# An encoder layer on one core: where a Strassen unit is split, when column sums are taken, which engine empties PSUM

## The chip, the cores and the metric

The kernel runs on one core of one Trainium2 chip. The metric is the time of one execution on the device in microseconds (us). The chip's engines work side by side, each through its own queue in order: TensorE (PE: matmuls; PEld: its weight loads), VectorE (DVE), ScalarE (ACT), GpSimd (POOL) and SyncE (SP, which issues most DMAs). They wait for each other by semaphores.

## The reference

One encoder layer over 512 tokens of width 1024, in float32. `ffn1` and `ffn2` have an inner width of 2816, 22 tiles of 128.

```python
h = h + 0.5 * swiglu(rms_norm(h, g_ffn1), w_ffn1_gate, w_ffn1_up, w_ffn1_down)
u = rms_norm(h, g_mix) @ w_in
h = h + concat([mla(u), diff_attention(u)]) @ w_out      # 8 + 4 heads
h = h + 0.5 * swiglu(rms_norm(h, g_ffn2), w_ffn2_gate, w_ffn2_up, w_ffn2_down)
gate = sigmoid(rms_norm(h, g_ple_in) @ w_ple_gate + b_ple_gate)
h = h + gate * rms_norm(p @ w_ple_proj, g_ple_out)       # p: 512 x 256, the "embedding"
```

## The kernel before

Activations lie transposed: 8 tiles `h[m]` of 128 features x 512 tokens. A float32 product is made of three matmuls (`mm3`, L407): each operand is split into a high part, a cast on ScalarE (`cast`), and a low part, the rest, a subtraction on VectorE (`low`, recorded at L97; where the helper `split` makes both, L93 and L94). High x high, high x low and low x high are summed in PSUM; these are the matmul lines L408, L409 and L410.

**The feed-forward block** (`ffn`, L590) goes through its 22 inner tiles in four groups (`FGROUPS`). Group 0 has four plain tiles: for each a gate and an up projection of 24 matmuls each, then `evac` (L598: scaling, Silu, product, and the split into `ht`), then the down projection (`ps_d`) for the 8 output tiles m; of the first three (`heads`, L668) all but the last tile's share is done ahead. Groups 1 to 3 have six tiles each, worked in pairs by `seven` (L550): one level of Strassen's scheme, seven products `r` of 256 columns in place of eight. Its weight side, a `Unit` (L135), needs sums of weight blocks: loads `ra`, `rb`, `rc`; two accumulating DMAs on POOL's queue (`sums`); then eleven steps in all of casts and lows to `xa`, `xb`, `xc`, `xs`, with two additions on POOL (L174, L175). Its activation side, `Forms` (L491), is made in group 0 by `build`, a generator that is advanced a few steps at a time beside the projections: per half, four products `y`, two POOL subtractions (`n1`, `n3`, L523 and L524), the splits `sa` of the four `y`, and the splits `fm` of four forms N1, T2, N3, N4, with `t2_` (L529) and `n4` (L532) made on VectorE.

**The order of the work.** In these blocks the program order on PE, DVE, ACT and POOL is kept as it is written (`manual_schedule`); in the attention only PE's is, and the scheduler places the rest. All weights of the kernel stand in one list, `items`: a `Chunk` (one tile: cast, low) or a `Unit`. `nxt` hands out the next finished one and frees the one used before. `slot(us)` spends a budget of VectorE time on the next steps of the list (`advance`, which stops when three tiles of a pool are held: `held`), and it stands at given places between the matmuls, ahead of the evacuation of the product just made; `load_ahead` issues loads while fewer than three raw tiles are in flight. The first unit of the next group is cut in two `Part`s of one and four steps (`cut`, L220), put among the down chunks, so that its sums start early. In group 0 both parts stand between the second and the third of four down chunks, and the four steps (`cast_a`, `low_a`, `cast_b`, `low_b`) come up in the slot behind the up projection of the last plain tile (L653), ahead of its `evac`.

**The column sums of the embedding.** `embed` (L964) makes p @ w_ple_proj in the attention, eight tiles of 6 matmuls; each leaves PSUM by a vector copy into a t2 tile (L981) and goes to DRAM by a POOL DMA (L982). A table, `FILL_STEPS`, says after which attention step a tile is made: 6, 8, ... 20 in this kernel. The tiles `pT` (the split p) stay in four t2 tiles of 16 until the last. In FFN2, `pe_norm` (L473) loads the eight tiles back (`pel`), squares them on ScalarE, adds the squares on POOL (`pe_acc`, L354), and at its last step takes the column sums by eight small matmuls (`ps_ss`, L364). It is advanced by two steps after each m of group 1's down projection (L701), so that its last step comes after m = 5.

**The end.** The gate is made in eight tiles; `evac_gate` (L1263) is three vector operations, a sigmoid and the store. The last tile is made in three pieces of 256, 128 and 128 columns (L1287).

Of the kernel before, what the change touches and what calls it, by code (L numbers as in the profile page):

```python
# [8 lines left out]
F32 = mybir.dt.float32  # L9
# [6 lines left out]
S = 512  # L16
DM = 1024
KT = DM // P
TT = S // P
# [16 lines left out]

FILL_PRE = "TTTTTTTTTTTTTKTKTKTTT"
FILL_MID = "TKK"
FILL_STEPS = ("T", "TTE", "TT", "TT", "T", "") + ("E", "") * 8
HEADS = "DDMDMDMMMMMM"  # L40

GC = {"ffn1": 0, "mix": 8, "ffn2": 16, "ple_in": 24, "ple_out": 32, "b_ple": 40,
# [7 lines left out]
def encoder_layer(ctx, tc, xT, pT, wst, gcols, rows, consts, out):  # L50
    nc = tc.nc
# [24 lines left out]
    def t2(name, dt=F32):  # L76
        return scope["t2p"].tile([P, S], dt, tag="t2", name=name)

    def page(name, shape=(P, 2, S), dt=F32R, pool=None):
        return (pool or pgp).tile(list(shape), dt, tag="pg", name=name)  # L80
# [8 lines left out]
    UP = (768, 768, BLK)  # L89
    st = {"off": P * sum(UP), "raws": 0, "time": 0.0}  # L90

    def split(dst_h, dst_l, src):
        nc.scalar.copy(dst_h, src)  # L93
        nc.vector.tensor_sub(dst_l, src, dst_h.bitcast(F32))  # L94

    def sub(dst_l, src, dst_h):
        nc.vector.tensor_sub(dst_l, src, dst_h.bitcast(F32))  # L97
# [114 lines left out]
    items = []  # L212

    def ffn_items():
        first_unit = None
        for gi, (f0, n, plain) in enumerate(FGROUPS):
            if plain:
                items.extend(Chunk(BLK) for _ in range(2 * n))
                down = [Chunk(2 * n * P) for m in range(0, KT, 2)]
                cut = 2, 2  # L220
            else:
                items.extend(first_unit if u == 0 else Unit(1 - u % 2) for u in range(n))
                down = [Chunk(n * P, 1 if m < KT // 2 else 0) for m in range(KT)]
                cut = 6, 7
            if gi < len(FGROUPS) - 1:
                first_unit = Unit(1)
                early_ = Part(first_unit, 1, 2), Part(first_unit, 4, 0)
                down.insert(cut[1], early_[1])
                down.insert(cut[0], early_[0])
            items.extend(down)  # L230
# [34 lines left out]
        load_ahead()  # L265
        return True

    def slot(us):

        st["time"] = us  # L270
        load_ahead()
        while st["time"] > 0 and (not any(isinstance(it, Unit) for it in ready)
                                  or isinstance(items[-1], Unit) and len(items[-1].steps) == 11) and advance():
            pass

    def steps(n):
# [214 lines left out]
    class Forms:  # L491
# [10 lines left out]
        def build(self, kp):  # L502
            def v(t):
                return t.rearrange("p (a b) -> p a b", b=HS)

            def put(i, src):
                pg_ = page(f"fm{i}")
                d = pg_.rearrange("p x (a b) -> p x a b", b=HS)
                split(d[:, 0], d[:, 1], src)
                self.pg[kp][i] = pg_  # L510

            held[1] += 1
            y = hl_tile(1, "y", F32)
            ks = (2 * kp, 2 * kp + 1, 2 * kp + 4, 2 * kp + 5)
            for i, k in enumerate(ks):
                nc.vector.scalar_tensor_tensor(out=y[:, i // 2, (i % 2) * S:(i % 2 + 1) * S], in0=h[k],
                                               scalar=g(self.name, k), in1=self.rbc, op0=ALU.mult, op1=ALU.mult)
                yield
            q = [y[:, i].rearrange("p (a b) -> p a b", b=S) for i in range(2)]
            b11, b12 = q[0][:, :, :HS], q[0][:, :, HS:]  # L520
            b21, b22 = q[1][:, :, :HS], q[1][:, :, HS:]
            n1, t2_, n3, n4 = [v(t2(f"f{i}")) for i in range(4)]
            nc.gpsimd.tensor_sub(n1, b11, b12)  # L523
            nc.gpsimd.tensor_sub(n3, b12, b22)  # L524
            for i, k in enumerate(ks):
                self.sa[k] = page(f"sa{k}")
                split(self.sa[k][:, 0, :], self.sa[k][:, 1, :], y[:, i // 2, (i % 2) * S:(i % 2 + 1) * S])
                yield
            nc.vector.tensor_add(t2_, b22, n1)  # L529
            put(self.N1, n1)  # L530
            yield
            nc.vector.tensor_sub(n4, b21, t2_)  # L532
            put(self.T2, t2_)
            yield
            put(self.N3, n3)
            yield
            put(self.N4, n4)
            held[1] -= 1
            yield
# [50 lines left out]
    def ffn(norm, after, side=None, early=None):  # L590
# [46 lines left out]
        for gi, (f0, n, plain) in enumerate(FGROUPS):  # L637
            hts = []
            if plain:
                late = []  # L640
                for f in range(n):
                    if f == 0 and early is not None:
                        psg, psu = early
                    else:
                        psg = psum("ps_g")
                        proj(psg, nxt(), norm.act)
                        slot(5.4)
                        if f == 1:
                            st_["r4"] = col_rsqrt(norm.acc, DM)
                        build(2)  # L650
                        psu = psum("ps_u")
                        proj(psu, nxt(), norm.act)
                        slot(3.5)  # L653
                    late.append((psg, psu, hts))
                    if f == 1:
                        st_["rbc"] = row_bcast(st_["r4"])
                        forms = Forms(norm.name, st_["rbc"])
                        builder = (x for kp in range(2) for x in forms.build(kp))
                    if f > 0:
                        for e in late:  # L660
                            evac(*e)
                        late = []
                        build(3 if f == 1 else 4)
            else:
                build(99)
                for f in range(0, n, 2):
                    pair(hts)
            heads = []  # L668
            if plain:

                w = nxt()
                for m in range(3):
                    if m == 2:
                        while not ready:
                            advance()
                        w = ready[0].out
                    heads.append(psum("ps_d"))
                    proj(heads[m], w, hts, m % 2 * n, range(n - 1))
                    slot(1.3)
                    build(1)  # L680
                w = used[0].out
            for m in range(KT):
                if not plain:
                    ps = psum("ps_d")
                    proj(ps, nxt(), hts)
                else:
                    if m % 2 == 0 and m > 0:
                        w = nxt()
                    if m < 3:
                        ps = heads[m]  # L690
                        proj(ps, w, hts, m % 2 * n, range(n - 1, n))
                    else:
                        ps = psum("ps_d")
                        proj(ps, w, hts, m % 2 * n)
                slot(0.0 if plain and m < 2 else 0.68 * n - (2.2 if gi == len(FGROUPS) - 1 else 0.75))
                nc.vector.scalar_tensor_tensor(out=h[m], in0=ps, scalar=0.5, in1=h[m],
                                               op0=ALU.mult, op1=ALU.add)
                last = gi == len(FGROUPS) - 1
                if last:
                    after(m)  # L700
                elif side is not None and gi == 1:  # L701
                    for _ in range(2):
                        next(side, None)
                build(1 if m < 2 else 2)
# [259 lines left out]
    def embed():  # L964
        pa = []
        for k in range(2):
            pt_ = t2("pT")
            nc.sync.dma_start(out=pt_, in_=pT[k])
            ah, al = t2("pTh", F32R), t2("pTl", F32R)
            split(ah, al, pt_)  # L970
            pa.append((ah, al))
        yield
        for m in range(KT):
            if m % 4 == 0:
                w = chunk()
            ps = psum("ps_pe")
            for k in range(2):
                c = slice(((m % 4) * 2 + k) * P, ((m % 4) * 2 + k + 1) * P)
                mm3(ps, w[:, 0, c], w[:, 1, c], pa[k][0], pa[k][1], k == 0, k == 1)
            pe = t2("pe")  # L980
            nc.vector.tensor_copy(out=pe, in_=ps)  # L981
            nc.gpsimd.dma_start(out=pe_dram[m], in_=pe)  # L982
            yield

    side = cols()
# [298 lines left out]
            evac_gate(*e)  # L1284
        pend = []
    w = nxt()
    for c in (slice(0, 256), slice(256, 384), slice(384, 512)):  # L1287
        ps = psum("ps_pg")
        for k in range(KT):
            b = slice(k * P, (k + 1) * P)  # L1290
            mm3(ps[:, c], w[:, 0, b], w[:, 1, b], n3.act[k][:, 0, c], n3.act[k][:, 1, c], k == 0, k == KT - 1)
        evac_gate(KT - 1, ps, c)
# [112 lines left out]
```

## Time and profile before

| | us |
|---|---|
| three runs: median (lowest to highest) | 1062.23 (1060.98 to 1063.0) |
| the profiled execution | 1061.28 |
| its span, first to last instruction | 1059.5 |
| PE busy in the span | 1026.2 |
| DVE busy | 762.8 |
| ACT busy | 524.3 |
| POOL busy | 325.1 |

A profile shows when each instruction of one execution began and how long it took. "Idle before" is the time for which its engine had nothing running ahead of it, and the releaser is the instruction that ended the wait. The granted clock is TensorE's: 1.00 is 2.4 GHz, 0.50 is 1.2 GHz. Matmuls overlap in their records (0.39 us for one of 512 columns), so a pitch is read from start to start. Where a row says x3, three instructions are merged and the duration is from the first start to the last end.

### The profile page before, as it was taken

What the parts mean: (1) busy time and instruction counts of PE and PEld (TensorE: products, weight loads), DVE (VectorE), ACT (ScalarE), POOL (GpSimd) and SP (SyncE); (2) the same over time, 40 slices, a digit from 0 to 9 for tenths busy, and PEclk for the clock granted to TensorE, in tenths of its full rate; (3) what the DMA queues carried; (4) which work ended last, traced back from release to release, by engine and by line L of the source; (5) the groups of instructions that cost most, each with busy time, mean ns of one, the idle gap of its engine ahead of it and who ended that gap; (6) DMA issues with size and microseconds to landing.
All of it is one profiled execution on the core that took longest, in us unless ns stands there. A gap on an engine that the chain in (4) does not pass through costs nothing.

```text
span 1059.5 us, 16005 instructions
## 1 busy us (share of the span) xinstructions
PE 1026.2 (97%) x6100; PEld 899.0 (85%) x6100; DVE 762.8 (72%) x1277; ACT 524.3 (49%) x891; POOL 325.1 (31%) x283
## 2 busy tenths in 40 slices
PE   9969999999999999999999999979997999999998
PEld 7859998998999898876667888769986998999877
DVE  7778855886586659778798763898854875587764
ACT  7435533543354457577687543445542562344441
POOL 1233412432341300036553221234415531352000
PEclk9989999999999999999899999989998999999999
DMA  6245654755563541321111123346574655565321
GB/s 242 99 121 163 158 164 110 181 149 167 132 160 118 170 163 60 96 79 51 60 49 62 41 81 98 95 114 160 142 218 119 154 143 180 140 160 180 120 100 50
DMA packets 50461, 133.76 MB, mean 126 GB/s; under 512 B 5872, under 2 KB 6896, under 8 KB 50384
## 3 DMA queue, kind: packets, MB, share of 16 engines
q1 hardware_dynamic: 37008, 106.88, 30.2%
q0 software_dynamic: 11792, 23.47, 12.7%
q10 hardware_dynamic: 1584, 2.39, 0.6%
q8 instruction: 48, 0.79, 0.3%
q14 instruction: 29, 0.24, 0.1%
HBM read 126.02 MB, written 6.29 MB: 125 GB/s over the span
## 4 chain that ended last, share of the span: by engine, by line
PE 81%; DVE 8%; ACT 4%; DMA 4%; issue 2%; POOL 1%; SPq 0%; ACTq 0%; DVEq 0%; POOLq 0%
PE r L410 11%; PE r L408 11%; PE r L409 11%; PE ps_d L408 7%; PE ps_d L409 6%; PE ps_d L410 6%; PE ps_in L408 2%; PE ps_in L410 2%; PE ps_in L409 2%; DVE hl L97 1%; PE ps_pt L1160 1%; PE ps_wo L408 1%; PE ps_wo L410 1%; PE ps_wo L409 1%; PE ps_pg L409 1%
## 5 line engine op out<-in xcount | busy, mean ns | idle before, releaser
L97 DVE TENSOR_TENSOR hl<-raw,hl 128x1024 fp32r<-128x1024 f32 (+4 forms) x110 | 121.4, 1116 | 69.2 <-ACT hl L124 66.9
L408 PE MATMUL ps_d<-ht,hl 128*128 128x512 f32 x352 | 140.3, 398 | 13.5 <-ACT ht L93 13.5
L124 ACT CAST hl<-raw 128x1024 fp32r<-128x1024 f32 (+2 forms) x104 | 96.4, 942 | 98.6 <-DMA raw<-in_wst_dram 28.8
L410 PE MATMUL ps_d<-ht,hl 128*128 128x512 f32 x352 | 139.1, 395 | 1.8 <-DVE hl L97 1.8
L409 PE MATMUL ps_d<-ht,hl 128*128 128x512 f32 x352 | 139.5, 396 | 0.0
L174 POOL TENSOR_TENSOR ra<-ra,rb 128x512 f32<-128x512 f32 x36 | 48.3, 1341 | 224.2 <-DVE xa L97 216.2
L408 PEld LDWEIGHTS ps_d<-ht,hl 128*128 128x128 f32 x352 | 67.6, 192 | 28.1 <-ACT ht L93 14.3
L410 PEld LDWEIGHTS ps_d<-ht,hl 128*128 128x128 f32 x352 | 67.4, 192 | 16.8 <-DVE hl L97 2.6
L408 PE MATMUL r<-sa,xa 128*128 128x256 f32 x288 | 81.5, 283 | 0.0
L409 PE MATMUL r<-sa,xa 128*128 128x256 f32 x288 | 81.5, 283 | 0.0
L410 PE MATMUL r<-sa,xa 128*128 128x256 f32 x288 | 81.5, 283 | 0.0
L408 PE MATMUL r<-fm,xb 128*128 128x256 f32 x288 | 81.5, 283 | 0.0
L409 PE MATMUL r<-fm,xb 128*128 128x256 f32 x288 | 81.5, 283 | 0.0
L410 PE MATMUL r<-fm,xb 128*128 128x256 f32 x288 | 81.5, 283 | 0.0
L409 PEld LDWEIGHTS ps_d<-ht,hl 128*128 128x128 f32 x352 | 67.6, 192 | 14.7 <-DVE ht L94 0.9
L175 POOL TENSOR_TENSOR ra<-ra 128x512 f32<-128x512 f32 x36 | 75.0, 2084 | 2.8
L97 DVE TENSOR_TENSOR xa<-ra,xa 128x1024 fp32r<-128x1024 f32 x36 | 44.3, 1231 | 38.7 <-ACT xa L162 38.7
L157 POOL DMA_DIRECT2D rb<-in_wst_dram x36 | 31.7, 882 | 110.7 <-DMA rb<-in_wst_dram 89.2
L97 DVE TENSOR_TENSOR xb<-rb,xb 128x1024 fp32r<-128x1024 f32 x36 | 63.1, 1753 | 0.0
L408 PEld LDWEIGHTS r<-sa,xa 128*128 128x128 f32 x288 | 55.3, 192 | 0.0
L409 PEld LDWEIGHTS r<-sa,xa 128*128 128x128 f32 x288 | 55.3, 192 | 0.0
L410 PEld LDWEIGHTS r<-sa,xa 128*128 128x128 f32 x288 | 55.3, 192 | 0.0
(335 smaller groups left out, 3047.3 us busy)
## 6 DMA issues: line engine op xcount, KB each, us to landing
raw<-in_wst_dram SPq DMA_DIRECT2D x52, 512.0 KB, 3.5
rb<-in_wst_dram SPq DMA_DIRECT2D x36, 512.0 KB, 3.8
ra<-in_wst_dram SPq DMA_DIRECT2D x36, 512.0 KB, 3.5
raw<-in_wst_dram SPq DMA_DIRECT2D x48, 384.0 KB, 3.1
rc<-in_wst_dram SPq DMA_DIRECT2D x36, 256.0 KB, 4.7
rb<-in_wst_dram POOLq DMA_DIRECT2D x36, 256.0 KB, 4.9
rc<-in_wst_dram POOLq DMA_DIRECT2D x36, 256.0 KB, 5.8
h<-in_xT_dram SPq DMA_DIRECT2D x8, 256.0 KB, 4.8
```

The costliest lines, as they stand in the source:

```text
L97: nc.vector.tensor_sub(dst_l, src, dst_h.bitcast(F32))
L124: nc.scalar.copy(self.hl[:, 0, :self.n], self.raw[:, :self.n])
L157: nc.gpsimd.dma_start(out=self.rb[:, self.LO], in_=self.s1[:, self.HI], accum_op=ALU.add)
L174: nc.gpsimd.tensor_add(ra[:, LO], ra[:, LO], self.rb[:, LO])
L175: nc.gpsimd.tensor_add(ra[:, HI], ra[:, HI], ra[:, LO])
L408: MM(ps, lhsT=wh, rhs=ah, start=start, stop=False, **kw)
L409: MM(ps, lhsT=wh, rhs=al, start=False, stop=False, **kw)
L410: MM(ps, lhsT=wl, rhs=ah, start=False, stop=stop, **kw)
L1160: nc.tensor.transpose(out=ps[:, qt * P:(qt + 1) * P], in_=u.prs[qt][:, kt * P:(kt + 1) * P], identity=ident)
```

## The change

- `FILL_STEPS`: the embedding's tiles 6 and 7 are made at steps 33 and 34 of the attention in place of 18 and 20. All eight leave PSUM by a ScalarE copy into half a page of the page pool (27 pages), in place of a vector copy into a t2 tile.
- `cut`: the four-step part of the next group's first unit stands one chunk later, between the third and the fourth down chunk of group 0. The slot behind the up projection of the last plain tile makes no steps of a part that has more than one left.
- `build`: the low of the fourth `sa` of each half, and `n4`, are made by GpSimd.
- The slot ahead of the very last `h` update of each feed-forward block is left out.
- `pe_norm` is advanced by two steps after m = 0 to 4 of group 1, and its last step comes after m = 3 of group 2.
- The gate's last tile is made in two pieces of 256 columns.

```diff
-FILL_STEPS = ("T", "TTE", "TT", "TT", "T", "") + ("E", "") * 8
+FILL_STEPS = ("T", "TTE", "TT", "TT", "T", "") + ("E", "") * 6 + ("",) * 15 + ("E", "E")
...
-    def split(dst_h, dst_l, src):
+    def split(dst_h, dst_l, src, eng=nc.vector):
         nc.scalar.copy(dst_h, src)
-        nc.vector.tensor_sub(dst_l, src, dst_h.bitcast(F32))
+        eng.tensor_sub(dst_l, src, dst_h.bitcast(F32))
...
-                cut = 2, 2
+                cut = 2, 3
...
-    def slot(us):
+    def slot(us, splits=True):
...
         while st["time"] > 0 and (not any(isinstance(it, Unit) for it in ready)
-                                  or isinstance(items[-1], Unit) and len(items[-1].steps) == 11) and advance():
+                                  or isinstance(items[-1], Unit) and len(items[-1].steps) == 11) \
+                and (splits or not isinstance(items[-1], Part) or len(items[-1].steps) == 1) and advance():
             pass
...
             for i, k in enumerate(ks):
-                self.sa[k] = page(f"sa{k}")
-                split(self.sa[k][:, 0, :], self.sa[k][:, 1, :], y[:, i // 2, (i % 2) * S:(i % 2 + 1) * S])
+                a = self.sa[k] = page(f"sa{k}")
+                split(a[:, 0, :], a[:, 1, :], y[:, i // 2, (i % 2) * S:(i % 2 + 1) * S], nc.gpsimd if i == 3 else nc.vector)
                 yield
...
-            nc.vector.tensor_sub(n4, b21, t2_)
+            nc.gpsimd.tensor_sub(n4, b21, t2_)
...
-                        slot(3.5)
+                        slot(3.5, f < n - 1)
...
-                slot(0.0 if plain and m < 2 else 0.68 * n - (2.2 if gi == len(FGROUPS) - 1 else 0.75))
+                if gi < len(FGROUPS) - 1 or m < KT - 1:
+                    slot(0.0 if plain and m < 2 else 0.68 * n - (2.2 if gi == len(FGROUPS) - 1 else 0.75))
...
-                elif side is not None and gi == 1:
+                elif side is not None and (gi == 1 and m < KT // 2 + 1 or gi == 2 and m == 3):
                     for _ in range(2):
                         next(side, None)
...
-            pe = t2("pe")
-            nc.vector.tensor_copy(out=pe, in_=ps)
+            if m % 2 == 0:
+                pg_ = page("pe", dt=F32)
+            pe = pg_[:, m % 2, :]
+            nc.scalar.copy(pe, ps)
             nc.gpsimd.dma_start(out=pe_dram[m], in_=pe)
...
-    for c in (slice(0, 256), slice(256, 384), slice(384, 512)):
+    for c in (slice(0, S // 2), slice(S // 2, S)):
```

## Rows read from the trace of the kernel before

**Rows 1.** The page's first part: busy us, share of the span, instructions.

```profile
PE 1026.2 (97%) x6100; PEld 899.0 (85%) x6100; DVE 762.8 (72%) x1277; ACT 524.3 (49%) x891; POOL 325.1 (31%) x283
```

**Rows 2.** Waits of PE: waiting line, releaser, total us, times, longest us.

```profile
PE ps_d L408 <- ACT ht L93: 13.5, 2, 7.5
...
PE ps_o L1046 <- ACT pt L93: 1.6, 1, 1.6
PE ps_ds L1103 <- DVE pe L981: 1.2, 1, 1.2
```

**Rows 3.** Timeline of PE at FFN1's heads: start us, us, instruction, idle before.

```profile
53.63 0.50 PE L410 MATMUL ps_d<-ht,hl 128*128 128x512 f32 x1 [0.88 <-DVE hl L97]
...
67.17 0.79 PE L408 MATMUL ps_d<-ht,hl 128*128 128x512 f32 x1 [7.54 <-ACT ht L93]
...
70.88 0.40 PE L410 MATMUL ps_d<-ht,hl 128*128 128x512 f32 x1
```

**Rows 4.** Timeline of DVE ahead of the last `ht`, FFN1 and FFN2.

```profile
61.09 1.22 DVE L97 TENSOR_TENSOR xa<-ra,xa 128x1024 fp32r<-128x1024 f32 x1 [4.57 <-ACT xa L162]
...
64.75 1.72 DVE L605 TENSOR_TENSOR v<-a,v 128x512 f32<-128x512 f32 x1
...
689.80 1.23 DVE L97 TENSOR_TENSOR xa<-ra,xa 128x1024 fp32r<-128x1024 f32 x1 [2.91 <-ACT xa L162]
```

**Rows 5.** Windows: stretch, length, busy us by engine, granted clock, DMA, GB/s.

```profile
72.00:84.00 12.00, 12.00 (x54) 9.91 (x53) 12.00 (x17) 5.42 (x9) 4.18 (x4) 1.00 0.64 151
```

**Rows 6.** Timeline of DVE and POOL: three lows alone, two beside POOL.

```profile
49.35 1.89 DVE L94 TENSOR_TENSOR sa<-y,sa 128x512 fp32r<-128x512 f32 x3
...
73.20 2.38 DVE L94 TENSOR_TENSOR sa<-y,sa 128x512 fp32r<-128x512 f32 x2
...
73.35 1.68 POOL L524 TENSOR_TENSOR f<-y 128x512 f32<-128x512 f32 x1 [0.63 <-DVE y L516]
```

**Rows 7.** Timeline of DVE and PE where FFN1's first product begins.

```profile
84.45 1.28 DVE L97 TENSOR_TENSOR xs<-ra,xs 128x512 fp32r<-128x512 f32 x2
...
85.18 0.39 PE L410 MATMUL r<-fm,xs 128*128 128x256 f32 x1
```

**Rows 8.** Timeline of PE and DVE at the column sums in FFN2.

```profile
800.07 0.39 PE L410 MATMUL ps_d<-ht,hl 128*128 128x512 f32 x1
806.35 1.86 PE L364 MATMUL ps_ss<-cst,pe_acc 128*128 128x1 f32 x8 [5.90 <-POOL pe_acc L354]
...
817.89 0.28 PE L408 MATMUL r<-fm,xs 128*128 128x256 f32 x1
...
803.43 3.41 DVE L97 TENSOR_TENSOR xs<-ra,xs 128x512 fp32r<-128x512 f32 x2
```

**Rows 9.** Timeline of the gate's last tile; DMA issues: KB each, us to landing.

```profile
1046.56 0.28 PE L408 MATMUL ps_pg<-act_ple_in,hl 128*128 128x256 f32 x1
...
1049.43 0.22 PE L408 MATMUL ps_pg<-act_ple_in,hl 128*128 128x128 f32 x1
...
1054.63 0.28 PE L410 MATMUL ps_pg<-act_ple_in,hl 128*128 128x128 f32 x1
...
1050.63 0.42 DVE L1267 TENSOR_TENSOR ga<-ga,pe 128x256 f32<-128x256 f32 x1 [0.58 <-ACT ga L1266]
1055.70 0.29 DVE L1267 TENSOR_TENSOR ga<-ga,pe 128x128 f32<-128x128 f32 x1 [0.47 <-ACT ga L1266]
...
out_dram<-ga SPq DMA_DIRECT2D x7, 256.0 KB, 2.0
out_dram<-ga SPq DMA_DIRECT2D x1, 128.0 KB, 3.4
out_dram<-ga SPq DMA_DIRECT2D x2, 64.0 KB, 1.6
```

**Rows 10.** Timeline of DVE at an embedding tile; the window behind it, as above.

```profile
503.50 0.69 DVE L981 COPY pe<-ps_pe 128x512 f32<-128x512 f32 x1 [1.16 <-POOL dpr L1121]
...
505.00:510.00 5.00, 5.00 (x16) 3.40 (x13) 3.75 (x16) 3.29 (x9) 1.52 (x4) 0.50 0.16 62
```

## The prediction

> **What bounds the kernel now.** I read the page first: the tensor engine is busy 97% of the span, so a change gains only where TensorE stands still or works without need [rows 1]. The second view is the list of waits, for TensorE alone. The reader is to see how short it is: 13.5 us in two waits of `ps_d` for ScalarE's cast of `ht`, 5.9 us of `ps_ss` for POOL's `pe_acc`, 1.6 and 1.2 us in the attention [rows 2, 8]. The third view is the timeline of each engine around each wait, to see what is queued ahead of the late instruction.
>
> The two waits for `ht` are the end of the plain group of each feed-forward block (FFN). The larger is 7.54 us, so the other is 13.5 - 7.5 = 6.0; TensorE comes out of it at its lower clock, 1.2 GHz: from 67.17 to 70.88 it starts 8 matmuls further, 3.71 us where the full pitch of 0.227 gives 1.81, so 1.9 are lost on top [rows 3]. VectorE shows the cause: ahead of `evac` of the last tile stand the two lows of the next unit, `xa` and `xb`, and `xa` waits 4.57 us (2.91 in FFN2) for a cast that waits for its load [rows 4]. But then VectorE has no gap at all: 12.00 us busy of 12 from 72 to 84 [rows 5]. And the first Strassen product starts when VectorE's low of `xs` is done: the third matmul of `r` at 85.18, the low at 84.45 plus 0.64 [rows 7]. So in this stretch the tensor engine's stall is not the bound; VectorE's queue is.
>
> **The change, part by part.**
>
> *Column sums one group later.* At 806.35 TensorE has waited 5.90 us for `pe_acc` [rows 8]. With `ps_ss` gone from there, the 36 matmuls of m = 6 and 7 follow the last one, which started at 800.07: 800.30 + 36 x 0.227 = 808.5. What is late next? The low of the last weight chunk comes ahead of the two lows of `xs`, and these end at 803.43 + 3.41 = 806.8 [rows 8], before 808.5, so the first `r` can start at 808.5 in place of 817.89: 9.4 us. The ScalarE squares, POOL's seven adds and the eight `pel` loads on SP stay where they are; only the eight small matmuls, three tiny vector and POOL operations and the copy move, to m = 3 of group 2, where `pe_acc` has long been done. There they cost TensorE the time of eight small matmuls, at most the 1.86 that they take here and by their full-clock pitch about half; I take 0.9. Gain 8.5, between 7.5 and 9.4. One t2 tile of ten is held through group 2; I see no wait on those tiles there and count nothing, with 1 us as its far end.
>
> *No split beside the last plain tile, the unit one chunk later, two subtractions to GpSimd.* I sum VectorE's queue from the first low of `sa` at 49.35 to the low of `xs`. The lows of `xa` and `xb` go behind `evac` and the builds, beside the head products; their loads are then long in, so the idle 4.57 us goes (2.91 in FFN2) [rows 4]. The evac of the last tile comes 4.57 + 2 x 1.2 + 1.04 = 8.0 us earlier (the wait, the two lows, and the vector operation that POOL's addition holds at 64.75), less 1.0 for what follows here: `ht` at about 60.2 instead of 67.2, and the heads end at 59.5, so the 7.54 us go as a wait for `ht`. On the other side four subtractions per FFN (the low of the fourth `sa` and `n4`, for two halves) leave VectorE, 4 x 0.60 = 2.4 us less (three such lows take 1.89 [rows 6]). But each now runs on POOL, and the trace shows what that does: with POOL's subtraction at 73.35, two vector lows take 2.38 us in place of 1.28, so one was held 1.10 us [rows 6]. Four of them: 4.4 - 2.4 = 2.0 us more. The same holds for the unit's two POOL additions: today only the second holds a vector instruction (1.72 for 0.68 at 64.75, [rows 4]), since the first lies beside reads of PSUM; among the lows of `sa` both do, another 1.1. Sum for FFN1: 4.57 - 2.0 - 1.1 = 1.5 us; for FFN2: 2.91 - 3.1 = -0.2. TensorE's own side costs a little of it: `n4` and the fourth low stand ahead of the low of the first down chunk, for which the heads wait 0.88 us already [rows 3], and the last down chunk is split behind them all. I take 1.0 for FFN1 and -0.2 for FFN2, together 0.8. The far ends: if POOL never holds VectorE, 4.57 + 2.4 - 1.1 = 5.9 and 2.91 + 2.4 - 1.1 = 4.2, together 10.1; if every resumption of TensorE comes at the lower clock, 1.9 less in each FFN, so -3.0.
>
> The Trainium skill (SBUF — State Buffer, section "Who interferes with whom") says that a VectorE instruction with two SBUF inputs and a GpSimd instruction that reads SBUF exclude each other, the later one for the whole instruction. The trace agrees in kind: `evac`'s reads of PSUM run beside POOL, subtractions from SBUF do not. By it each of the four would hold VectorE for all of POOL's 1.68 us, which is the third rival below.
>
> *The gate's last tile in two pieces.* Its second half is 48 matmuls of 128 columns from 1049.43 to 1054.63, a pitch of 0.111; the first half's 24 of 256 columns took from 1046.56 to 1049.43, a pitch of 0.120 [rows 9]. So 128 columns cost nearly what 256 do: 48 x 0.111 - 24 x 0.120 = 2.45 us less. Behind the last matmul come three vector operations at 0.42 for 0.29 and one sigmoid: 0.5 more [rows 9]. The last store is 128 KB for 64 KB; one of 64 lands in 1.6 us, one of 256 in 2.0, but the one of 128 took 3.4 [rows 9]. I take 2.0. Gain 2.45 - 0.5 - 0.4 = 1.5, between 0.1 and 1.9.
>
> *Embedding tiles.* Eight PSUM copies of 0.6 us leave VectorE for ScalarE; twelve matmuls (2.7 us of TensorE) move from steps 18 and 20 to 33 and 34, their two DMA issues on POOL's queue with them; the output goes to a page, no longer to a t2 tile. TensorE waits 1.2 us for such a copy today; that copy itself came at 503.50 after 1.16 us on a POOL addition, and the clock is at its half for 505 to 510 [rows 2, 10]. The far end up is the wait and those 2.5 us, 3.7, with some around it 5. Against it: the four split tiles of `p` now hold four of 16 t2 buffers 14 steps longer, and four pages more are asked of a pool of 27. The nearest row for a missing buffer on the path is the `ps_o` wait, 1.6 us, which with a slow resumption of 1.9 makes -3.5. I take +1.0. Moving TensorE's 2.7 us is nothing by itself: the gap at `ps_o` is a chain behind a score product, which shifts along.
>
> *The last slot.* At the end of FFN2 the three weight tiles of its pool are held at m = 7, so the slot does nothing now; in FFN1 TensorE runs on without a wait. Zero, 0.3 either way.
>
> **Sum.** 8.5 + 0.8 + 1.5 + 1.0 = 11.8 us. The profiled execution took 1061.28 us for a span of 1059.5: 1049.5 by that. It lies 0.95 under the median of the three runs, 1062.23, from which the sum gives 1050.4. I say 1050.0.
>
> **Rivals.**
> 1. *The stall goes whole.* POOL's subtractions find VectorE waiting or reading PSUM, and both stretches come in by 5.9 and 4.2: 8.5 + 10.1 + 1.5 + 1.0 = 21.1, 1040.2. For it: the wait for `ht` is by far the largest in the list. Against it: VectorE is full from 72 to 84 [rows 5].
> 2. *Slower: t2 tiles run out in the attention.* With 12 buffers left instead of 16, every softmax step from 20 to 33 waits for a transposition two heads back, as one copy does today. Price: 13 steps x 1.2 us = 15.6, TensorE's wait in [rows 2]. It decides from ten such steps on (12 us against the other 10.8). At 13: 1061.28 - 10.8 + 15.6 = 1066. Against it: one step alone shows such a wait now, with the four tiles held as well.
> 3. *POOL holds VectorE for its whole instruction.* 4 x 1.68 - 2.4 = 4.3 instead of 2.0 in each FFN, 4.6 us less: 1054.1. For it: POOL's rows are as long as that; against it: 73.20 shows 1.10 held. The same place is reached if each new start of TensorE is at the lower clock.
> 4. *The move of the column sums gives the wait alone*, because another operand is late at 808: 5.9 for 8.5, 1052.4.
>
> **How the numbers follow.** The forecast has 0.62 (1046 to 1053 as its own range), rival 1 0.12, rival 3 0.12, rival 4 0.06, rival 2 0.04, and 0.04 for a few steps of it (1056 to 1060). For eight in ten I leave out the far tail of rival 1 and rival 2: 1042 to 1056. A measurement of this kernel tells about 0.2%, 2.1 us, from no change; only rival 2 and a part of its mild form come out over 1060: faster 0.92, same 0.04, slower 0.04.
>
> **What would show it.** Right: no wait for `pe_acc`, `r` of group 2 following `ps_d` directly; no wait for `ht` over 1 us, but TensorE idle in several pieces between 52 and 85 and the first `r` still at about 84, at the low of `xs`; vector lows of 1.7 us beside POOL's new subtractions; 24 gate matmuls of 256 columns at the end. Wrong: first `r` near 79, VectorE idle before it (rival 1); waits of `ps_pt` on `pr` in steps 20 to 34 (rival 2).

## The result, and the profile after

The changed kernel takes 1047.28 us, the median of four runs (1045.43 to 1048.2), beside 1062.62 for the kernel before in the same comparison: ratio 0.9849, 95% interval 0.9822 to 0.9877, or 15.3 us by the medians. The forecast was 1050.0, between 1042 and 1056. The profiled execution took 1048.2 us for a span of 1046.4; against 1061.28 that is 13.1 less, where the sum said 11.8.

In the changed kernel's page the first part stands against [rows 1]: TensorE busy 6.2 us less, POOL 12.1 more, VectorE 1.2 less.

```profile
PE 1020.0 (97%) x6076; PEld 895.0 (86%) x6076; DVE 761.6 (73%) x1258; ACT 526.7 (50%) x898; POOL 337.2 (32%) x291
```

Its waits of PE, beside [rows 2]: waiting line, releaser, total, times, longest. The 13.5 us for `ht` and the 5.9 for `pe_acc` are gone. In the place of the first stand 14.4 us in four waits for the low of a down chunk, two in each FFN, where two such waits of 0.9 were before.

```profile
PE ps_d L411 <- DVE hl L97: 14.4, 4, 4.8
PE ps_ss L365 <- ACT sqo L1142: 1.6, 1, 1.6
...
PE ps_o L1051 <- DVE pt L94: 0.6, 1, 0.6
```

The timeline of PE at FFN1's heads, which begin at 54.25, beside [rows 3, 7]. TensorE waits 2.46 for the first down chunk (0.88 before) and 4.72 for the last, and comes out of the second at the half clock: the next ones follow at 0.425 in place of 0.227. The first product `r` starts at 85.90.

```profile
57.33 0.50 PE L411 MATMUL ps_d<-ht,hl 128*128 128x512 f32 x1 [2.46 <-DVE hl L97]
...
78.70 0.79 PE L411 MATMUL ps_d<-ht,hl 128*128 128x512 f32 x1 [4.72 <-DVE hl L97]
...
85.90 0.28 PE L409 MATMUL r<-fm,xs 128*128 128x256 f32 x1
```

The timeline of VectorE in the same stretch, beside [rows 4, 7], and under it POOL's. There is no idle time from 68 to 86. The low of `sa` takes 1.77 beside POOL where it takes 0.68 alone, that of `xb` 2.32 for 1.21; the last down chunk (`hl`, 77.43) stands behind them. The first low of `xs` ends at 84.47 + 0.68 = 85.15, the second at 85.75. The rows at 52.66, 54.98, 75.76 and 80.37 are those that POOL's four new subtractions lengthen.

```profile
52.66 1.79 DVE L530 TENSOR_TENSOR f<-y,f 128x512 f32<-128x512 f32 x1
...
54.98 2.29 DVE L97 TENSOR_TENSOR hl<-raw,hl 128x1024 fp32r<-128x1024 f32 x1
...
68.41 1.21 DVE L97 TENSOR_TENSOR xa<-ra,xa 128x1024 fp32r<-128x1024 f32 x1
69.54 1.77 DVE L94 TENSOR_TENSOR sa<-y,sa 128x512 fp32r<-128x512 f32 x1
71.24 2.32 DVE L97 TENSOR_TENSOR xb<-rb,xb 128x1024 fp32r<-128x1024 f32 x1
73.48 1.75 DVE L94 TENSOR_TENSOR sa<-y,sa 128x512 fp32r<-128x512 f32 x1
...
75.76 1.15 DVE L94 TENSOR_TENSOR sa<-y,sa 128x512 fp32r<-128x512 f32 x1
...
77.43 1.21 DVE L97 TENSOR_TENSOR hl<-raw,hl 128x1024 fp32r<-128x1024 f32 x1
...
80.37 2.37 DVE L94 TENSOR_TENSOR fm<-f,fm 128x512 fp32r<-128x512 f32 x2
...
84.47 1.28 DVE L97 TENSOR_TENSOR xs<-ra,xs 128x512 fp32r<-128x512 f32 x2
```

```profile
68.56 2.21 POOL L525 TENSOR_TENSOR f<-y 128x512 f32<-128x512 f32 x1 [1.82 <-DVE y L517]
70.73 1.75 POOL L174 TENSOR_TENSOR ra<-ra,rb 128x512 f32<-128x512 f32 x1
72.56 2.13 POOL L175 TENSOR_TENSOR ra<-ra 128x512 f32<-128x512 f32 x1
74.65 1.71 POOL L94 TENSOR_TENSOR sa<-y,sa 128x512 fp32r<-128x512 f32 x1
```

The window of [rows 5] in the changed kernel (length, busy us of PE, PEld, DVE, ACT, POOL, granted clock, DMA share, GB/s) shows the two effects in one line: VectorE full, TensorE busy 7.28 of 12 at a mean clock of 0.72.

```profile
72.00:84.00 12.00, 7.28 (x23) 5.52 (x22) 11.92 (x14) 4.29 (x8) 7.65 (x6) 0.72 0.34 112
```

The column sums: PE at the end of group 1 in FFN2 and in group 2, beside [rows 8]. `r` follows the last `ps_d` at the full pitch, and the eight small matmuls take 0.95 in group 2, as forecast.

```profile
804.14 0.39 PE L411 MATMUL ps_d<-ht,hl 128*128 128x512 f32 x1
804.37 0.28 PE L409 MATMUL r<-fm,xs 128*128 128x256 f32 x1
...
881.77 0.95 PE L365 MATMUL ps_ss<-cst,pe_acc 128*128 128x1 f32 x8
```

The gate's last tile, PE and the stores, beside [rows 9]: 24 matmuls from 1035.62, 24 to 1041.26, and a store of 128 KB that lands in 1.7 us.

```profile
1035.62 0.28 PE L409 MATMUL ps_pg<-act_ple_in,hl 128*128 128x256 f32 x1
1038.50 0.28 PE L409 MATMUL ps_pg<-act_ple_in,hl 128*128 128x256 f32 x1
...
1041.26 0.28 PE L411 MATMUL ps_pg<-act_ple_in,hl 128*128 128x256 f32 x1
...
out_dram<-ga SPq DMA_DIRECT2D x2, 128.0 KB, 1.7
```

### The profile page after: what moved, and what is told of

The parts are those of the page before. It is cut to its first block, busy times and chain, and to the rows that moved or that the text cites. A ratio compares the mean times of both kernels' runs of the same rounds, so it can differ in the third digit from the quotient of the medians.

```text
span 1046.4 us, 15957 instructions
## 1 busy us (share of the span) xinstructions
PE 1020.0 (97%) x6076; PEld 895.0 (86%) x6076; DVE 761.6 (73%) x1258; ACT 526.7 (50%) x898; POOL 337.2 (32%) x291
## 4 chain that ended last, share of the span: by engine, by line
PE 77%; DVE 11%; DMA 4%; ACT 3%; issue 3%; POOL 1%; ACTq 0%; DVEq 0%; SPq 0%; POOLq 0%
PE r L411 10%; PE r L409 10%; PE r L410 9%; PE ps_d L411 7%; PE ps_d L409 7%; PE ps_d L410 6%; PE ps_in L409 2%; PE ps_in L411 2%; PE ps_in L410 2%; DVE hl L97 2%; DMA rb<-in_wst_dram 2%; PE ps_wo L409 1%; PE ps_wo L411 1%; PE ps_wo L410 1%; DMA raw<-in_wst_dram 1%
## 5 line engine op out<-in xcount | busy, mean ns | idle before, releaser
L97 DVE TENSOR_TENSOR hl<-raw,hl 128x1024 fp32r<-128x1024 f32 (+4 forms) x110 | 124.3, 1143 | 70.2 <-ACT hl L124 67.6
L411 PE MATMUL ps_d<-ht,hl 128*128 128x512 f32 x352 | 139.4, 396 | 14.4 <-DVE hl L97 14.4
L97 DVE TENSOR_TENSOR xb<-rb,xb 128x1024 fp32r<-128x1024 f32 x36 | 65.3, 1813 | 0.3 <-ACT xb L166 0.3
```

Source lines behind the costliest of these rows:

```text
L411: MM(ps, lhsT=wl, rhs=ah, start=False, stop=stop, **kw)
```

## The experiments

Twelve kernels. Four are the kernel before with one part of the change (e1, e9, e10, e11), two with half of one (e3, e4), six are the changed kernel with something undone or moved. Their stages, read from PE's timelines of one profile each, from the first matmul of a stage to the first of the next: "FFN heads" is from the heads to the end of group 1's products, "down 1" the down projection of FFN2's group 1 with what follows up to `r`, "last tile" from its first matmul to the end of the span.

| kernel | median us | ratio to before (95%) | FFN1 heads | attention | FFN2 heads | down 1 | last tile |
|---|---|---|---|---|---|---|---|
| before | 1062.62 | | 93.97 | 271.22 | 93.30 | 42.11 | 12.94 |
| changed | 1047.28 | 0.9849 (0.9822 to 0.9877) | 92.72 | 266.81 | 92.77 | 32.67 | 10.78 |
| e1 | 1058.81 | 0.9962 (0.9946 to 0.9977) | 92.15 | 269.08 | 91.35 | 43.24 | 12.75 |
| e2 | 1043.68 | 0.9818 (0.9799 to 0.9836) | 92.50 | 266.72 | 91.03 | 32.67 | 10.84 |
| e3 | 1062.04 | 0.9991 (0.998 to 1.0003) | 93.87 | 267.71 | 95.07 | 43.78 | 12.95 |
| e4 | 1062.43 | 1.0002 (0.9989 to 1.0016) | 93.20 | 269.74 | 92.87 | 43.34 | 12.79 |
| e5 | 1041.62 | 0.9832 (0.9811 to 0.9853) | 90.47 | 265.01 | 90.51 | 32.66 | 10.83 |
| e6 | 1043.26 | 0.984 (0.9826 to 0.9855) | 91.93 | 266.56 | 92.40 | 32.67 | 10.81 |
| e7 | 1041.96 | 0.9832 (0.9814 to 0.9851) | 90.18 | 268.09 | 90.19 | 32.67 | 10.78 |
| e8 | 1033.17 | 0.9749 (0.9731 to 0.9766) | 87.41 | 264.69 | 87.51 | 32.66 | 10.83 |
| e9 | 1051.84 | 0.991 (0.9894 to 0.9925) | 93.77 | 270.21 | 93.18 | 32.67 | 12.82 |
| e10 | 1059.82 | 0.9969 (0.9954 to 0.9985) | 93.22 | 266.31 | 93.26 | 43.46 | 12.83 |
| e11 | 1059.85 | 0.9979 (0.9967 to 0.9991) | 93.32 | 270.06 | 92.84 | 42.65 | 11.27 |
| e12 | 1037.82 | 0.9777 (0.9757 to 0.9797) | 88.63 | 266.38 | 89.91 | 32.67 | 10.85 |

The kernel before was timed afresh beside the experiments, at 1062.4 (with e1 to e4), 1060.4 (with e5 to e8) and 1062.4 (with e9 to e12); so kernels of different groups are compared by their ratios.

By these stages the 13.1 us of the changed kernel's profile are 9.4 in down 1, 4.4 in the attention, 2.2 in the last tile, 1.3 and 0.5 in the two FFN heads; against them stand 1.0 in group 2, where the small matmuls now are, 2.1 in the start-up ahead of FFN1's heads and 1.6 in the gate up to its last tile. The last two are no part of the change: the start-up takes 52.1 to 54.6 us in the fourteen profiles whatever the edits, and the gate is told in the last section.

A second table has the two ends that meet at group 1's first product: where the first low of `xs` ends, which is VectorE's end, and where the third matmul of `r` starts, which is the first that needs it (in e5 below it is the one that waits). Both are in us behind the first matmul of the heads, FFN1 and FFN2, worked out from the timelines.

| kernel | first low of `xs` ends | third matmul of `r` starts |
|---|---|---|
| before | 32.99, 31.34 | 33.04, 32.47 |
| changed | 30.90, 30.92 | 31.89, 31.92 |
| e1 | 29.48, 29.51 | 31.31, 30.50 |
| e2 | 29.44, 29.51 | 31.66, 30.21 |
| e5 | 29.49, 29.53 | 29.55, 29.58 |
| e6 | 27.92, 27.96 | 31.09, 31.57 |
| e7 | 27.92, 27.93 | 28.06, 27.99 |
| e8 | 25.17, 25.26 | 25.22, 25.31 |
| e12 | 26.79, 26.89 | 27.80, 29.05 |

Apart from the kernel before, whose idle time before `xa` differs between the FFNs, VectorE's end repeats to 0.1 us from one FFN to the other. Where the second figure is more than 0.1 above the first, TensorE came later than VectorE, and it varies: behind the wait for the last down chunk e2 starts 12 matmuls at a pitch of 0.425 in FFN1 and 5 in FFN2.

**e1, the moved unit alone.** The kernel before with

```diff
-                cut = 2, 2
+                cut = 2, 3
...
-                        slot(3.5)
+                        slot(3.5, f < n - 1)
```

> The kernel before with one part of the change alone: the four-step part one chunk later and the slot behind the last plain tile kept free of it; GpSimd makes no new subtraction. Theory V (VectorE's queue bounds the stretch up to the first Strassen product): the idle 4.57 and 2.91 us of VectorE go, less 1.1 each for the second addition that now holds a vector low, so the stretch from the heads to the first r is 3.5 us shorter in FFN1 (32.6 to 29.1) and 1.8 in FFN2 (32.2 to 30.4); the whole 5.3 under the kernel before, ratio 0.9950. Rival T (TensorE's own next wait, for the low of the last down chunk, takes the place of the wait for ht): the wait moves and keeps its size, stretches and time within 1 us of the kernel before.

Measured 4.0 us less by the ratio (2.4 to 5.7), so theory V and not T. VectorE's end came 3.51 and 1.83 us sooner, which are theory V's 3.5 and 1.8. But T's wait is there, as the waits of PE show: `ht` is gone from them and the last down chunk is waited for 5.0 us. TensorE is now the later end, and the third matmul of `r` comes 1.7 and 2.0 sooner, where 3.5 and 1.8 were said.

```profile
PE ps_d L411 <- DVE hl L97: 11.8, 4, 5.0
```

**e2, GpSimd's part undone.** The changed kernel with

```diff
-                split(..., nc.gpsimd if i == 3 else nc.vector)
+                split(..., nc.vector)
...
-            nc.gpsimd.tensor_sub(n4, b21, t2_)
+            nc.vector.tensor_sub(n4, b21, t2_)
```

> The changed kernel with the fourth low of sa and n4 back on VectorE; all else as changed. Theory V with the hold (each of POOL's four new subtractions holds a vector instruction 1.1 us and saves it 0.6): the stretch from the heads to the first r is 2.0 us shorter in each FFN than in the changed kernel (31.7 to 29.7), the first heads wait falls from 2.46 us to about 0.9, the whole is 3 to 4 us under the changed kernel, ratio to the kernel before about 0.982. Rival R (GpSimd relieves VectorE): 2.4 us more in VectorE's queue, the stretches 1 to 2.4 us longer, the whole 2 to 5 us over the changed kernel, ratio about 0.989.

0.9849 - 0.9818 = 0.0031 under the changed kernel, 3.3 us (3.6 by the medians). The intervals of the two ratios meet, but all four times of e2 (1042.5 to 1044.0) lie under the four of the changed kernel: theory V, and this part of the change made the kernel slower. VectorE's end came 1.46 and 1.41 us sooner, where 2.0 was said; `r` came 0.2 sooner in FFN1, where TensorE was late, and 1.7 in FFN2. The first heads wait is back at 0.83:

```profile
54.43 0.50 PE L411 MATMUL ps_d<-ht,hl 128*128 128x512 f32 x1 [0.83 <-DVE hl L97]
...
76.46 0.79 PE L411 MATMUL ps_d<-ht,hl 128*128 128x512 f32 x1 [5.00 <-DVE hl L97]
```

VectorE runs eight instructions more than in the changed kernel (page: 1266 for 1258) and is busy 2.1 us less (759.5 for 761.6).

**e3 and e4, the halves of the embedding's part.** The kernel before, e3 with the first and e4 with the second:

```diff
-            pe = t2("pe")
-            nc.vector.tensor_copy(out=pe, in_=ps)
+            if m % 2 == 0:
+                pg_ = page("pe", dt=F32)
+            pe = pg_[:, m % 2, :]
+            nc.scalar.copy(pe, ps)
...
-FILL_STEPS = ("T", "TTE", "TT", "TT", "T", "") + ("E", "") * 8
+FILL_STEPS = ("T", "TTE", "TT", "TT", "T", "") + ("E", "") * 6 + ("",) * 15 + ("E", "E")
```

> The kernel before with the embedding tiles copied out of PSUM by ScalarE into a page, at the same steps of the attention as before. Theory C (the changed kernel's 4.4 us in the attention come from the copy): the wait of 1.2 us for a copy and the half-clock spell behind it go, the attention is 3 to 5 us shorter, ratio 0.996. Rival S (they come from moving two tiles to steps 33 and 34): within 1 us of the kernel before, and the spell behind the copies stays.

> The kernel before with the embedding tiles 6 and 7 made at steps 33 and 34, still copied by VectorE into t2 tiles. Theory C: none of the waiting copies belongs to the moved tiles, so the wait and the half-clock spell stay, within 1 us of the kernel before, ratio 0.999 to 1.001. Rival S: 3 to 5 us less, ratio 0.996. My rival of t2 tiles running out: pT's four tiles are held 14 steps longer with the copies still in t2 tiles, so waits of ps_pt on pr from step 20 to 34, over 5 us more.

By the times neither does anything that can be told (e3: 2.1 less to 0.3 more), so theory C's 3 to 5 us did not come. In e3's profile the wait for the copy is gone and the attention takes 267.7 us, where the kernels with the old embedding (before, e1, e9, e11) take 269.1 to 271.2; but the wait of 1.63 for `ps_o` stays, one of 1.1 on `dpr` is new, and that profile's FFN2 is 1.8 longer than before's, its wait for `ht` 8.1 us: the load of `ra` took 6.9 us to land, 4.7 in the kernel before. In e4 the wait for the copy stays (1.91), the one for `ps_o` is gone, and one of 1.64 for `sqo` has come; no wait of `ps_pt` on `pr` shows, so e4's rival of t2 tiles running out is not seen. e10 tries both halves.

**e9, e10, e11, the other parts alone.** The kernel before with the edit of `side` (e9), of both lines above (e10), of the gate's pieces (e11), as in the diff of the change.

> The kernel before with one part of the change alone: the column sums of the embedding one group later. My sum's term: the 5.9 us wait, its 1.86 us of small matmuls and the slow resumption go, 0.95 comes back in group 2; 8.5 us less, ratio 0.9920. Profiles of kernels with the old place since taken show group 1's down stretch at 42.1 to 43.8 us where 32.7 is its length without the wait, so up to 10.1 less, ratio 0.9905. Rival (the wait alone goes): 5.9 less, ratio 0.9945.

> The kernel before with both embedding edits, the ScalarE copy into a page and the tiles 6 and 7 at steps 33 and 34. If the attention's gain of the changed kernel (271.2 to 266.8 in the profiles) is this part's: attention at 265 to 268 us, 2 to 4 us under the kernel before, ratio 0.9965 to 0.998. Rival (the kernel of e3 and e4 timed at 0.9991 and 1.0002, and the difference of the profiles is chance of the clock): 0.999 to 1.000.

> The kernel before with the gate's last tile in two pieces, nothing else. My sum's term: 1.5 us less. From the first matmul of the last tile to the end of the span it is 12.9 us before and 10.8 in the changed kernel, so 2.1 less, ratio 0.9980. Rival (a longer last store and evacuation give it back): 0 to 0.4 less, ratio 0.9996 to 1.0.

By the ratios 9.6, 3.3 and 2.2 us less. The embedding's part came out at more than either half, though the intervals of e3 (up to 2.1) and e10 (from 1.6) meet. Its windows, first e10, then the kernel before:

```profile
500.00:510.00 10.00, 10.00 (x54) 6.94 (x53) 8.81 (x27) 6.42 (x17) 5.25 (x8) 1.00 0.25 88
...
530.00:540.00 10.00, 8.41 (x42) 6.73 (x41) 7.84 (x23) 6.87 (x16) 3.71 (x5) 0.83 0.00 1
...
560.00:570.00 10.00, 9.37 (x55) 7.48 (x54) 9.73 (x18) 8.09 (x18) 2.07 (x3) 1.00 0.23 80
```

```profile
500.00:510.00 10.00, 8.80 (x35) 5.98 (x32) 6.64 (x20) 5.29 (x13) 4.84 (x6) 0.71 0.24 79
530.00:540.00 10.00, 10.00 (x59) 6.37 (x55) 9.24 (x27) 8.97 (x20) 4.25 (x4) 1.00 0.24 79
560.00:570.00 10.00, 8.28 (x41) 6.58 (x40) 7.25 (x16) 6.06 (x13) 3.96 (x6) 0.83 0.14 53
```

The granted clock is the seventh figure from the length on: 0.71 at 500 and 0.83 at 560 before, with the wait for the copy and the 1.63 us for `ps_o` ahead of them; in e10 both windows are at 1.00, the `ps_o` wait is 0.60, and one new spell stands at 530, behind a wait of 1.59 for `sqo`. Two spells at the lower clock have become one here, but these vary: e1, e9 and e11 have one each with the old embedding, the changed kernel one, e8 none. What is steady are the waits. The gaps of TensorE over 0.22 us in the attention sum to 4.2 (before), 4.7 (e1), 4.8 (e9) and 5.7 us (e11), to 3.7 and 5.1 with the halves (e3, e4), and to 2.8 in e10 and 2.5 in the changed kernel and in e2.

**e5, e6, e7, the order in VectorE's queue.** The kernel of e2 with, in e5, the updates of `h` for m = 0 and 1 behind the slot of m = 2:

```diff
+                if plain and m < 2:
+                    pre.append((m, ps))
+                    continue
...
+                for m_, ps_ in pre + [(m, ps)]:
                     nc.vector.scalar_tensor_tensor(out=h[m_], in0=ps_, ...)
+                    if m_ < m:
+                        build(1)
```

in e6 the last forms behind the first product, with `y` released as soon as `n4` is made (e7 has both edits):

```diff
+        if rest is not None:
+            rest()
...
-            seven(forms, gate)
+            seven(forms, gate, lambda: build(99))
...
-                build(99)
...
-                build(1 if m < 2 else 2)
+                build(1 if m < 2 else 2 if m == 2 else 0)
```

> The kernel of e2 with one order changed: the updates of h for m = 0 and 1 (and the build steps behind them) stand behind the slot of m = 2, so the low of the last down chunk comes 2.4 us earlier in VectorE's queue. Theory D (two ends meet at the first r of group 1: TensorE's down products behind its wait for that low, and VectorE's queue up to the low of xs, in e1's FFN2 711.28 and 711.1): TensorE's wait falls from 5.0 to 2.6 us but r starts no sooner, since the low of xs stays where it is; within 1 us of e2, 1043 to 1044.5. Rival P (TensorE's wait and its slow resumption alone set the start of r): 2.4 us and up to 1.7 of clock in each FFN, 5 to 8 us under e2, 1036 to 1039.

> The kernel of e2 with the last two forms (N3 and N4 of the second half, two casts and two lows) made behind the first product r, and the update of h for m = 3 behind the low of xs. Theory D: the low of xs comes 1.9 us sooner, but TensorE's down products end where they did; within 1 us of e2. Rival Q (VectorE's queue alone sets the start of r): 1.9 us in each FFN, 3.8 under e2, about 1040.

> Both edits of e5 and e6 at once. Theory D: both ends move, r starts 1.9 us sooner in each FFN, 3 to 4 us under e2, 1039.7 to 1040.7, more than e5 and e6 together. Rivals P and Q: the sum of e5 and e6, whichever has the gain.

Neither order alone nor both can be told from e2 by the ratios (0.9832, 0.984 and 0.9832 against 0.9818). In the stages e5 gains 2.0 in FFN1 and 0.5 in FFN2, e7 2.3 and 0.8, e6 0.6 in one and loses 1.4 in the other. Theory D names the two ends rightly: in e5 VectorE's end stays where it is in e2, the wait for the chunk is down to 2.61, and then `r` waits for `xs` in its third matmul. But it took the ends for level. In e2 TensorE was later by 2.2 and 0.7 us, so `r` did come sooner in e5, its third matmul by 2.1 and 0.6. The clock still falls behind the shorter wait, to a pitch of 0.425 for seven matmuls. In e6 VectorE's end comes 1.5 sooner and `r` stays with TensorE, so rival Q is out.

```profile
74.54 0.50 PE L411 MATMUL ps_d<-ht,hl 128*128 128x512 f32 x1 [2.61 <-DVE hl L97]
...
75.42 0.63 PE L411 MATMUL ps_d<-ht,hl 128*128 128x512 f32 x1
...
82.95 0.39 PE L411 MATMUL r<-fm,xs 128*128 128x256 f32 x1 [1.26 <-DVE xs L97]
```

Theory D's 3 to 4 us for both edits did not come. With the first matmul of `r` 3.6 and 2.7 us earlier in e7's FFNs than in e2's (by the distance from the heads), group 1's products take 1.3 and 1.9 us longer: TensorE waits 0.69 for the next unit's `xs` there, which it did not before.

**e8 and e12, no POOL arithmetic beside VectorE.** To e7 (e8) and to e2 (e12):

```diff
-            nc.gpsimd.tensor_sub(n1, b11, b12)
-            nc.gpsimd.tensor_sub(n3, b12, b22)
+            nc.vector.tensor_sub(n1, b11, b12)
+            nc.vector.tensor_sub(n3, b12, b22)
...
-            nc.gpsimd.tensor_add(ra[:, LO], ra[:, LO], self.rb[:, LO])
-            nc.gpsimd.tensor_add(ra[:, HI], ra[:, HI], ra[:, LO])
+            self.add.tensor_add(ra[:, LO], ra[:, LO], self.rb[:, LO])
+            self.add.tensor_add(ra[:, HI], ra[:, HI], ra[:, LO])
...
+                if plain:
+                    first_unit.add = nc.vector
```

> The kernel of e7 with the other POOL subtractions and additions of the stretch on VectorE too: n1 and n3 of both halves and the two additions of the first unit. Theory V (each holds a vector instruction 1.1 us while it runs, and takes VectorE 0.6 itself): in the second half four of them, 4 x (1.1 - 0.6) = 2.0 us less ahead of the low of xs; r 2 us sooner in each FFN where TensorE follows, 2 to 4 us under e7. Rival R: what POOL does is for nothing to VectorE, 2.4 us more in its queue, 3 to 5 us over e7.

> The kernel of e2 (the changed kernel with its new POOL subtractions on VectorE) with n1, n3 and the first unit's two additions on VectorE too, and no change of the order: e8 without the edits of e5 and e6. Theory V (POOL's instructions hold VectorE 1.1 us each): the low of the last down chunk and the low of xs both come 2 us sooner in each FFN, so r 2 to 3 us sooner, 4 to 6 us under e2, ratio 0.976 to 0.978. Rival O (e8's gain needs the new order): within 1 us of e2, ratio 0.981 to 0.983.

Theory V in both: VectorE's end comes 2.7 us sooner than in e7 in each FFN of e8, and 2.6 sooner than in e2 in each of e12, where 2.0 was said. e8 takes 1033.17 us, 0.0083 of the ratio (8.8 us) under e7, where 2 to 4 were forecast; e12 0.0041 (4.4 us) under e2, within its forecast. The stages that the edit touches give 5.5 us in e8 and 5.0 in e12; what else e8 gained lies in the start-up, the attention and the gate, where the edit changes nothing and e8's profile has no matmuls at the lower clock ahead of the gate's end. Why the clock held there is not shown. e8 beats both kernels: 0.9749 to the one before, some 1% under the changed one. VectorE's timelines, e7 first, then e8, show how: two additions now stand in its queue, and the queue is shorter.

```profile
68.39 1.78 DVE L94 TENSOR_TENSOR sa<-y,sa 128x512 fp32r<-128x512 f32 x1
70.09 2.32 DVE L97 TENSOR_TENSOR xb<-rb,xb 128x1024 fp32r<-128x1024 f32 x1
72.33 1.75 DVE L94 TENSOR_TENSOR sa<-y,sa 128x512 fp32r<-128x512 f32 x1
```

```profile
66.61 0.68 DVE L94 TENSOR_TENSOR sa<-y,sa 128x512 fp32r<-128x512 f32 x1
67.21 1.22 DVE L97 TENSOR_TENSOR xb<-rb,xb 128x1024 fp32r<-128x1024 f32 x1
68.35 0.68 DVE L174 TENSOR_TENSOR ra<-ra,rb 128x512 f32<-128x512 f32 x1
69.06 0.69 DVE L175 TENSOR_TENSOR ra<-ra 128x512 f32<-128x512 f32 x1
69.67 0.69 DVE L94 TENSOR_TENSOR sa<-y,sa 128x512 fp32r<-128x512 f32 x1
```

From the start of the low of `sa` to the end of the next one it is 5.69 us in e7 and 3.75 in e8, though e8 has 1.3 us of additions in it. TensorE follows. In e8's PE timeline the wait for the last chunk is 0.79, and `r` starts 24.49 us behind the heads (53.17) in place of 27.82; no slice of its page is under a granted clock of 0.9.

```profile
71.55 0.50 PE L413 MATMUL ps_d<-ht,hl 128*128 128x512 f32 x1 [0.79 <-DVE hl L97]
...
77.66 0.39 PE L411 MATMUL r<-fm,xs 128*128 128x256 f32 x1 [0.82 <-ACT xs L187]
```

And VectorE's busy time in the pages of e7 and e8 falls by 5.3 us with 12 instructions of 0.6 us more, so 12.5 us of holding are gone, 1.04 for each:

```profile
PE 1020.4 (98%) x6076; PEld 894.5 (86%) x6076; DVE 759.9 (73%) x1266; ACT 526.5 (51%) x898; POOL 325.9 (31%) x283
```

```profile
PE 1014.2 (98%) x6076; PEld 888.7 (86%) x6076; DVE 754.6 (73%) x1278; ACT 526.7 (51%) x898; POOL 299.9 (29%) x271
```

## Why the prediction was right, and where its sizes were off

The parts run alone add up, in us by their ratios at 1062.4: 9.6 (e9), 3.3 (e10), 2.2 (e11), and 4.0 - 3.3 = 0.7 for the unit and GpSimd (e1, less what e2 won back), 15.8; the change as a whole has 0.0151, 16.0. Each part has an interval of 1.3 to 3.5 us either way, so that they meet this closely is in part luck. Against them the sum's terms:

- **Column sums, 8.5: measured 9.6.** The mechanism was right in each step: no wait, `r` right behind `ps_d`, the low of `xs` done in time (801.7), 0.95 paid in group 2. The size came from the profile with the shortest such stretch: down 1 took 42.11 us there and 42.65 to 43.78 in five later profiles with the old place. Rival 4 (a gain of 5.9) is out; its 1052.4 should read 1052.1 by the sum that the other rivals use.
- **Unit and GpSimd, 0.8: measured 0.7.** A difference of 4.0 and 3.3 is not known to better than some 4 us, so the match is luck; what the runs show are the halves. The idle time gone: VectorE's end 3.51 and 1.83 sooner in e1, as forecast, and 4.0 of 5.3 us in the time, since TensorE was then late. POOL's four subtractions: forecast 2.0 in each FFN, 1.4 by VectorE's end in e2, and 3.3 of 4.0 in the time. In the timeline of FFN1 they hold VectorE 1.11, 1.07, 0.47 and 1.09 us, 3.74 in all, less the 2.4 that they save: 1.3. Four full holds were counted, and one is short. Rival 3's price (four times 1.68) and rival 1 (no hold) are out by these rows. The prediction misread the 1.68: it is POOL's record at 73.35, and over half a microsecond of it is POOL's own wait for the vector low of 73.20 (see the last section). The split between the FFNs was rougher than the sum: by the distance from the heads to the first matmul of `r`, 1.0 for FFN1 and 0.55 for FFN2, where -0.2 was said.
- **"TensorE's stall is not the bound; VectorE's queue is"** was too short. Two ends meet at `r`, and in the changed kernel TensorE was the later: the first low of `xs` was done at 85.15, but the last of the 22 matmuls behind the 4.72 us wait began at 85.67, kept back by the lower clock, and the third matmul of `r` at 86.13, 1.0 us behind VectorE's end in both FFNs. So `r` did not start at the low of `xs`, as the signs of being right have it. The last down chunk, which the prediction saw behind the subtractions but gave no price, is what TensorE waited for, 4.7 and 4.8 us; with 2.5 each for the first chunk these are the 14.4, where 13.5 and 1.8 stood before. e5 shortened that end and `r` then waited for `xs`. VectorE's queue sets both, through the last down chunk and through `xs`, but the clock behind the wait comes on top.
- **The gate's last tile, 1.5: measured 2.2** (1.0 to 3.5). The matmuls gave what was said; the store of 128 KB lands in 1.7 us, where I had taken 2.0 between 1.6 and 3.4. That the changed kernel's whole gate shows 0.6 only in the profile is the clock: up to its last tile it took 42.4 us for 40.8.
- **Embedding, 1.0: measured 3.3** (1.6 to 4.9), the largest error, and a matter of size. I had the wait and the low clock behind it at 3.7 and the far end at 5, and took 1.0 to leave room for full t2 pools, of which no run shows a sign: rival 2's waits of `ps_pt` on `pr` are absent. By the sums of the gaps 1.4 to 3.2 us are waits: those for the copies went (the longest is 1.2 to 1.9 with the old embedding, in the place of [rows 10]) and 1.0 of the 1.63 for `ps_o`, less the 1.59 for `sqo` that came. The rest would be the clock behind them, which differs from profile to profile; that is argued, not shown. e3 alone, with its new wait on `dpr` and the one for `ps_o` still there, has gaps of 3.7; whether that is why its times show almost nothing stays open.

Three of four terms were too small, together by 4 us, within what the range allowed for.

## What to carry to other kernels

Before work is given to GpSimd to relieve VectorE, look for a place where VectorE reads PSUM or idles; beside SBUF arithmetic a subtraction that VectorE does in 0.6 us held it for up to 1.1, and taking such work back, even where it had long stood there, was the best edit of this study. Price a wait of TensorE with the lower clock behind it, and look for the operand that is next in the same vector queue before counting the wait as gained: the product starts at the later of the two ends. Where a term rests on one wait in one profile, look for how much that wait varies.

## What the runs showed of the hardware

POOL and VectorE take turns by whole instructions. In the kernel before POOL's second addition begins with no vector instruction on SBUF in its way, and lasts 1.26:

```profile
64.66 1.26 POOL L175 TENSOR_TENSOR ra<-ra 128x512 f32<-128x512 f32 x1
```

It ends at 65.92, and VectorE's `v`, issued at 64.75 [rows 4], ends 0.55 behind it. In the changed kernel's rows POOL's addition of 70.73 ends at 72.48 and the low of `xb` (71.24) 1.08 behind it, at 73.56; POOL's next (72.56) ends 1.13 behind that, at 74.69, and the low of `sa` (73.48) 0.54 behind that. So POOL's instruction of 512 columns takes 1.1 to 1.3 us itself. Its records of 1.7 to 2.2 hold, ahead of that, its own wait for the vector instruction that came first; and VectorE's hold is 1.1 us whether the low has 512 columns (1.78 for 0.68 in e7) or 1024 (2.32 for 1.21), or less where POOL had begun well before (0.47 at 75.76). The Trainium skill (SBUF — State Buffer, section "Who interferes with whom") says that the two exclude each other and that the later one waits for the whole instruction of the earlier; these rows agree. The figure to plan with is POOL's time without its own wait, 1.1 to 1.3 here, not the length of its record.

The stretch of the gate up to its last tile took 40.8 us in eight profiles and 42.4 in six, with the same short waits at its second tile (0.37 and 0.29). In the six longer ones TensorE then ran seven or eight matmuls at a pitch of 0.425, in the eight none. A microsecond and a half is so decided by the granted clock from one execution to the next.
